# Second parts of the down projection's weights by a negating copy on ScalarE and an accumulating DMA

## The chip, the cores and the metric

The kernel runs on one core of a Trainium2 chip. The metric is the device time of one execution in microseconds (us). The profile is one execution recorded by the hardware; times inside it count from the start of its span.

## The reference, cut to what matters

Two layers of an encoder over 768 tokens of width 1024 (512 of a prompt, 256 of a sample). Each layer is a feed-forward, a mixer (a state-space recurrence and neighbourhood attention in layer 0, windowed attention in layer 1), and a second feed-forward. So the feed-forward runs four times, with a hidden width of 2816:

```python
def swiglu(x, wg, wu, wd):
    return (jax.nn.silu(x @ wg) * (x @ wu)) @ wd

for layer in range(DEPTH):
    x = x + 0.5 * swiglu(rms_norm(x, norm_ffn[layer, 0]), ...)
    ...                                   # the mixer
    x = x + 0.5 * swiglu(rms_norm(x, norm_ffn[layer, 1]), ...)
return rms_norm(x, norm_final)
```

The change touches how `wd`, the down projection's weights, come to TensorE. All inputs are float32.

## The kernel before, in words

**Two parts for each operand.** TensorE works on float32r, a float32 rounded to fewer bits. To keep the accuracy, `split` (L85) turns a float32 tile into two float32r parts: ScalarE copies it, which rounds (the first part, L88), and VectorE subtracts that copy from the source (the second part, L89). Each product is then three matmuls: first by first, and each first by the other's second.

**Weights.** A weight block of 128 x 1024 float32 (512 KB) is loaded by a DMA on SyncE's queue (SP) into a buffer `raw` (7 of them, L77). `part` (L92) splits 512 columns of it into a buffer `whl` with both parts (8 of them, L93). `weights` (L97) is a generator that yields the parts of the whole network in the order in which they are used. `take` (L187) hands out the next part and `fetch` (L180) lets the generator run ahead (`self.look`). What really bounds the running ahead is the eight `whl` buffers: a part is split when TensorE has done with the part eight places before it.

**Feed-forward.** `ffn` (L225) goes through the 22 blocks of 128 hidden features in 11 pairs, numbered 0 to 10. For a pair, the gate product has seven or eight weight parts of 12 matmuls each (L247), the up product as many. `rows` (L349) then adds the pair's share of the down projection: it takes four parts, which this text calls d0 to d3 (d0 and d1 are the two halves of the columns for the first feature block, d2 and d3 for the second), and does 72 matmuls (L362), twelve for each of six token tiles: for the left half of the columns d0 three times and d2 three times, for the right half d1 and d3. The `rows` of a pair come after the next pair's gate, so that the order on TensorE is gate of pair b, `rows` of pair b-1, up of pair b. The `rows` of pair 0 of each feed-forward are an exception in that much other work precedes them at once. Each token tile's half is added to the residual by VectorE (L365).

**GpSimd (POOL).** In the first feed-forward only, GpSimd also builds the matrices of the recurrence (`s5_matrices`, L418) in 16 rounds: some twenty small products (L579 to L595), DMAs of the results to DRAM (L600, L623, L624), while TensorE transposes its results (L605) in between its own work. In the other three feed-forwards GpSimd has nothing but a tiny operation for each norm (L199).

**Order.** The program's order on each engine is fixed by a scheduler when the kernel is built; every engine works through its own list in order, and waits by semaphores. A change of one instruction can therefore change the order of its neighbours too.

Of the kernel before, what the change touches and what calls it, by code (L numbers as in the profile page):

```python
# [11 lines left out]
F32 = mybir.dt.float32  # L12
F32R = mybir.dt.float32r
I32 = mybir.dt.int32
AF = mybir.ActivationFunctionType
ALU = mybir.AluOpType
# [3 lines left out]
P = 128  # L20
# [17 lines left out]
# neighbourhood attention: (first query, queries, first key, keys) in the order (column, row)  # L38
NA_Q = [(0, 128, 0, 256), (128, 128, 64, 256), (256, 128, 192, 256), (384, 128, 256, 256),
        (512, 128, 512, 160), (640, 128, 608, 160)]  # L40
# key blocks (first key, keys) of the windows above
# [5 lines left out]
class Trunk:  # L47
# [20 lines left out]
    def warm(self, after):  # L68
        """have the table of the square root loaded as soon as the column "after" is there"""
        w = self.cp.tile([P, 1], F32, tag="warm", name="warm", bufs=2)  # L70
        self.nc.scalar.activation(w, after, AF.Sqrt, bias=self.one, scale=0.0)
# [13 lines left out]
    def split(self, hl, lo, src):  # L85
        """hl (rounded) + lo = src, exactly"""
        nc = self.nc
        nc.scalar.copy(hl, src)  # L88
        nc.vector.tensor_sub(lo, src, hl.bitcast(F32))  # L89

# [6 lines left out]
    def weights(self):  # L97
        """the weights of the whole trunk"""
        v = self.nc.vector

        def block(n, *at):
            r = self.raw(self.a[n][at])
            for e in range(2):
                yield (n, *at, e), self.part(r[:, e * 512 : (e + 1) * 512])

        def down(q, b):
            for c in (2 * b, 2 * b + 1):
                yield from block("w_down", q, c)

        def head(n, q, b, r1):  # L110
            for e in range(2):
                yield (n, q, b, f"1{e + 1}"), self.part(r1[:, e * 512 : (e + 1) * 512])

        def quad(n, q, b, r1=None):
            """the parts and sums of two blocks of features; without the head if r1, the first, is given"""
            k = lambda z: (n, q, b, z)
            headed, r1 = r1 is not None, self.raw(self.a[n][q, 2 * b]) if r1 is None else r1
            a11, a12 = r1[:, :512], r1[:, 512:]
            if not headed:
                yield k("11"), self.part(a11)  # L120
            r2 = self.raw(self.a[n][q, 2 * b + 1])
            a21, a22 = r2[:, :512], r2[:, 512:]
            s1 = self.wp.tile([P, 512], F32, tag="st", name="st", bufs=2)
            v.tensor_add(s1, a21, a22)  # L124
            v.tensor_sub(a21, a11, a21)
            v.tensor_sub(a11, s1, a11)
            yield k("s2"), self.part(a11)
            yield k("s1"), self.part(s1)
            if b < 2:
                yield k("22"), self.part(a22)  # L130
            yield k("s3"), self.part(a21)
            if not headed:
                yield k("12"), self.part(a12)
            v.tensor_sub(a12, a12, a11)
            yield k("s4"), self.part(a12)
            if b > 1:
                yield k("22"), self.part(a22)

        def fast(q):
            both = ("w_gate", "w_up")  # L140
            first = lambda n, b: self.raw(self.a[n][q, b])
            r = {n: first(n, 0) for n in both}
            for b in range(2):
                heads = [head(n, q, b, first(n, 2) if b else r[n]) for n in both]
                for z in heads * 2:
                    yield next(z)
            for z in [quad(n, q, 0, r[n]) for n in both] * 5:
                yield next(z)
            for b in range(1, NF // 2):
                for n in both:  # L150
                    yield from quad(n, q, b, first(n, 2) if b == 1 else None)
                    if n == "w_gate":
                        yield from down(q, b - 1)
            yield from down(q, NF // 2 - 1)

        def out(n, kb, half):
            for e in range(2):
                yield from block(n, half, 2 * kb + e)

        yield from fast(0)  # L160
        for f in [0, 1, 2, 3] + [4 + e + h for h in range(4) for e in (8, 0, 4)]:
            yield from block("w_in_even", f)
        yield from out("w_out_even", 1, 0)
        for f in range(2):
            yield from block("s5_wg", f)
        for kb, half in ((1, 1), (0, 0), (0, 1)):
            yield from out("w_out_even", kb, half)
        yield from fast(1)
        yield from fast(2)
        for f in (8, 9):  # L170
            yield from block("w_in_odd", f)
        for e in range(2):
            yield from block("w_v_odd", e)
        for f in range(8):
            yield from block("w_in_odd", f)
        for kb, half in ((0, 0), (0, 1), (1, 0), (1, 1)):
            yield from out("w_out_odd", kb, half)
        yield from fast(3)
# [16 lines left out]
    def norm_half(self, t, out):  # L195
        """sum of squares of the first half of token tile t"""
# [5 lines left out]
    def norm_rows(self, t, gb, out, ss, parts=1):  # L202
        """out = rms_norm of token tile t"""
# [4 lines left out]
        for e in range(parts):  # L208
            c = slice(e * DM // parts, (e + 1) * DM // parts)
# [8 lines left out]
    def gemm(self, o, w, act, k0, n, kk=range(KM), last=KM - 1):  # L218
        """o[128 features, n tokens] = w^T act, w stationary; w and act hold four blocks of 128 features to a tile"""
# [5 lines left out]
    def ffn(self, q, norm, tail, extra=None):  # L225
        """gate and up by Winograd's form of Strassen's product over 2 blocks of features, of inputs and of tokens"""
# [4 lines left out]
        with ExitStack() as ctx:  # L231
# [18 lines left out]
            def quad(n, b, use):  # L250
                """steps of the four blocks; use(feature block, token half, value)"""
# [97 lines left out]
    def rows(self, hs, q, b, pos, tail=None):  # L349
        """steps of x += 0.5 h wd over a pair of blocks of features"""  # L350
# [22 lines left out]
    def out_pass(self, name, kb, half, act, tail=None):  # L373
        """steps of x[:, half] += act w over k-block kb (4 of 128 features); act(part, k) has all tokens"""
# [24 lines left out]
    def fgemm(self, f, hn, evac, norm=None, kk=KM):  # L399
        """steps of a feature block of act @ w, feature-major; f names the weights, evac(psum, first token, tokens)"""  # L400
# [13 lines left out]
        h = kk // 2  # L414
        return [lambda: part(0, NP, NS, range(kk)), lambda: part(1, 0, NP, range(h)), lambda: part(2, 0, NP, range(h, kk))]

# [1 line left out]
    def s5_matrices(self, pool, spare):  # L418
# [10 lines left out]
        class Room:  # L429
            """carves blocks out of tiles"""  # L430
# [26 lines left out]
        def exp(out, x):  # L457
            """exp to float32's accuracy"""
# [51 lines left out]
        # (a - 1) / lambda  # L510
# [15 lines left out]
        # powers 0..8  # L526
# [40 lines left out]
        def start(q):  # L567
            """a pair of groups: W2 (state -> outputs), W1 (inputs -> state)"""
# [28 lines left out]
        def finish(q):  # L597
            """W1 transposed, E (inputs -> outputs)"""
# [44 lines left out]
    def mixer0(self, norm, tail):  # L643
# [4 lines left out]
        with ExitStack() as ctx:  # L648
            mp = ctx.enter_context(self.tc.tile_pool(name="mix0", bufs=1))

            # inputs of S5, in (chunk position, channel) rows
# [14 lines left out]
            def qkv(h):  # L666
                """steps of a head pair's values, queries and keys, in the order (column, row)"""
# [28 lines left out]
            def na(h):  # L696
                """steps of a head pair; q is overwritten by the output, feature-major"""
# [65 lines left out]
            # chunk inputs of the states; both directions run from slot to slot, the reversed one backwards in time  # L763
# [31 lines left out]
            # outputs of S5: chunk inputs through M, states before the chunk through W2  # L795
# [54 lines left out]
            # the neighbourhood half of the output projection around the gate of S5  # L850
# [25 lines left out]
    def mixer1(self, norm, tail):  # L876
        nc, a = self.nc, self.a
        hn = norm.hn
        with ExitStack() as ctx:
# [4 lines left out]
            # a key head's two parts above each other, the first part in the rows that its queries have  # L884
# [11 lines left out]
            # (query tile, first key tile, key tiles, first column of the bias)  # L896
# [20 lines left out]
            def att(m, store):  # L917
                """steps of the heads of key heads 2m and 2m+1"""
                bias, pend, pts, qq = [] if m else [bias0], {}, [], {}

                def queries(t):
                    """the first parts twice above each other, and the second parts"""
# [146 lines left out]
def weave(main, *sides):  # L1069
    """emit the steps of main with those of the sides spread between them"""  # L1070
# [13 lines left out]
class NormOut:  # L1084
    """final rms_norm, a token tile at a time"""
# [17 lines left out]
class NormT:  # L1103
    """rms_norm, transposed to feature-major in two parts, a token tile at a time"""
# [41 lines left out]
class NormS(NormT):  # L1146
    """the same as the sums that ffn multiplies with; tokens of tiles 4, 5, 0 and of 1, 2, 3 face each other"""
# [46 lines left out]
    def rest(self):  # L1194
        """the parts that later products take, a step for each"""
# [39 lines left out]
def _na_index(t):  # L1235
    """row of the padded table for each (query, key) of query tile t"""
# [9 lines left out]
def _layout(i):  # L1246
# [13 lines left out]
    # heads of the odd layer: tile (m, r) holds head r of key heads 2m and 2m+1  # L1260
# [5 lines left out]
    # S5  # L1266
# [11 lines left out]
    # biases by constant index; the last entry of the padded table is the masked one  # L1278
# [26 lines left out]
```

## Time and profile before

| | us |
|---|---|
| time, median of 2 runs | 2751.07 (2750.31 to 2751.83) |
| span of the profiled execution | 2751.6 |
| TensorE (PE) busy | 2695.9 (98%) |
| VectorE (DVE) busy | 2008.4 (73%) |
| ScalarE (ACT) busy | 1176.3 (43%) |
| GpSimd (POOL) busy | 340.6 (12%) |
| DMA: bytes moved | 217.48 MB |

The profiled execution's span stands 0.5 us above the median of the runs, so sums made against the span hold for the median as well. Busy time of PE is modelled for the ends of its pipelined matmuls, so it says where PE had work, not how close it is to its peak. PEclk is the clock that TensorE was granted, as a share of its 2.4 GHz; 0.5 is its lower level of 1.2 GHz.

### The profile page before, as it was taken

Reading aid. Unit: us, or ns where it says so; the run is one execution under the profiler, and the core shown is the slowest. Engines: PE = TensorE matmul, PEld = TensorE weight load, DVE = VectorE, ACT = ScalarE, POOL = GpSimd, SP = SyncE. Lnnn points to the kernel's source line nnn. Section 1 sums busy time; section 2 is a strip of 40 time slices with the busy share of each in tenths; the row PEclk is TensorE's granted clock in tenths of the full one; section 3 lists DMA queues with packets and bytes.
Section 4 is the critical chain, followed back from the end, with each engine's and each line's share of the span. In section 5 each row is a group of like instructions: output and inputs, shape, how many; then the busy total and the mean of one; then the engine's idle time right before and its main releaser. Section 6 shows DMA issues by size and latency. Waiting matters only on the chain.

```text
span 2751.6 us, 38966 instructions
## 1 busy us (share of the span) xinstructions
PE 2695.9 (98%) x14636; PEld 2422.3 (88%) x14636; DVE 2008.4 (73%) x3878; ACT 1176.3 (43%) x2464; POOL 340.6 (12%) x688
## 2 busy tenths in 40 slices
PE   7999999998999999999999999999999999999998
PEld 7988988888888999999989999999876689999997
DVE  8967776772964887677789776767557678777776
ACT  6333333343565633333354333334457664333333
POOL 0156654300840000000000000000000000000000
PEclk9999999999999999999999999999999999999999
DMA  4122222316244222121203121211201123122221
GB/s 155 65 90 85 90 90 77 127 54 134 89 125 142 81 81 85 54 85 54 88 29 122 62 77 62 79 61 39 100 16 39 45 72 108 63 76 68 71 70 54
DMA packets 81245, 217.48 MB, mean 79 GB/s; under 512 B 22848, under 2 KB 29632, under 8 KB 80800
## 3 DMA queue, kind: packets, MB, share of 16 engines
q1 hardware_dynamic: 77152, 203.91, 23.4%
q0 software_dynamic: 3904, 11.08, 1.2%
q8 instruction: 115, 1.88, 0.3%
q14 instruction: 74, 0.61, 0.1%
HBM read 199.17 MB, written 17.89 MB: 79 GB/s over the span
## 4 chain that ended last, share of the span: by engine, by line
PE 92%; DVE 3%; DMA 2%; ACT 2%; POOL 1%; issue 1%; SPq 0%; DVEq 0%; ACTq 0%; POOLq 0%
PE ps L247 44%; PE ps L362 25%; PE ps L222 8%; PE ps L389 5%; PE ps L957 1%; PE ps L990 1%; PE ps L956 1%; PE ps L978 1%; PE ps L1133 1%; PE ps L1009 1%; PE ps L774 1%; PE ps L616 1%; DVE raw L210 1%; PE ps L746 1%; DVE whl L89 0%
## 5 line engine op out<-in xcount | busy, mean ns | idle before, releaser
L88 ACT CAST whl<-raw 128x512 fp32r<-128x512 f32 x796 | 480.3, 621 | 943.7 <-PE ps L362 446.6
L247 PE MATMUL ps<-bt,whl 128*128 128x384 f32 x4224 | 764.6, 336 | 8.9 <-DVE ct L273 8.9
L247 PEld LDWEIGHTS ps<-bt,whl 128*128 128x128 f32 x4224 | 737.9, 189 | 12.5 <-DVE ct L273 10.1
L362 PE MATMUL ps<-whl,hl 128*128 128x512 f32 x3168 | 732.7, 391 | 0.0
L89 DVE TENSOR_TENSOR whl<-raw,whl 128x512 fp32r<-128x512 f32 x796 | 550.6, 705 | 220.2 <-ACT whl L88 209.2
L362 PEld LDWEIGHTS ps<-whl,hl 128*128 128x128 f32 x3168 | 593.9, 188 | 123.5 <-ACT hl L88 0.9
L247 PE MATMUL ps<-b,whl 128*128 128x384 f32 x3168 | 580.3, 336 | 0.0
L247 PEld LDWEIGHTS ps<-b,whl 128*128 128x128 f32 x3168 | 555.1, 189 | 3.5 <-ACT hct L617 0.3
L365 DVE SCALAR_TENSOR_TENSOR x<-ps,x 128x512 f32<-128x512 f32 x528 | 361.5, 689 | 217.5 <-PE ps L362 215.3
L199 POOL TENSOR_SCALAR ss<-ss 128x1 f32<-128x1 f32 x42 | 11.3, 270 | 1787.2 <-ACT raw L198 1787.2
L222 PE MATMUL ps<-hn,whl 128*128 128x256 f32 (+1 forms) x1248 | 231.2, 342 | 1.4 <-ACT hn L88 1.4
L222 PEld LDWEIGHTS ps<-hn,whl 128*128 128x128 f32 x1248 | 191.8, 190 | 31.8 <-issue 3.3
L88 ACT CAST hl<-hct 128x384 fp32r<-128x384 f32 x176 | 86.9, 512 | 50.8 <-DVE hct L317 44.9
L389 PE MATMUL ps<-whl,ob 128*128 128x512 f32 x432 | 105.2, 399 | 0.0
L89 DVE TENSOR_TENSOR hl<-hct,hl 128x384 fp32r<-128x384 f32 x176 | 98.3, 577 | 7.7 <-ACT hl L88 7.4
L389 PEld LDWEIGHTS ps<-whl,ob 128*128 128x128 f32 x432 | 80.7, 190 | 19.7 <-issue 2.2
L279 ACT COPY ct<-ps 128x384 f32<-128x384 f32 x88 | 42.3, 481 | 102.4 <-PE ps L247 102.4
L314 ACT ACTIVATE hct<-ct 128x384 f32<-128x384 f32 x88 | 46.3, 526 | 91.3 <-DVE ct L285 79.9
L284 DVE TENSOR_TENSOR ct<-ps,hct 128x384 f32<-128x384 f32 x88 | 48.9, 556 | 29.3 <-PE ps L247 29.1
L124 DVE TENSOR_TENSOR st<-raw 128x512 f32<-128x512 f32 x88 | 62.6, 712 | 10.1 <-DMA raw<-in_w_gate 9.2
L958 DVE CUSTOM_DVE_ANT_0 raw<-ps,gb,sk 128x256 f32<-128x256 f32 (+1 forms) x96 | 48.6, 525 | 29.0 <-PE ps L957 25.8
L392 DVE TENSOR_TENSOR x<-ps,x 128x512 f32<-128x512 f32 x48 | 33.0, 688 | 48.6 <-PE ps L389 48.6
(235 smaller groups left out, 2632.8 us busy)
## 6 DMA issues: line engine op xcount, KB each, us to landing
raw<-in_w_gate SPq DMA_DIRECT2D x92, 512.0 KB, 3.6
raw<-in_w_up SPq DMA_DIRECT2D x92, 512.0 KB, 3.6
raw<-in_w_down SPq DMA_DIRECT2D x88, 512.0 KB, 3.7
raw<-in_w_in_even SPq DMA_DIRECT2D x16, 512.0 KB, 3.6
raw<-in_w_in_odd SPq DMA_DIRECT2D x10, 512.0 KB, 4.8
W2d<-raw POOLq DMA_DIRECT2D x16, 256.0 KB, 2.4
W1d<-hct POOLq DMA_DIRECT2D x16, 256.0 KB, 3.0
raw<-W1d SPq DMA_DIRECT2D x8, 512.0 KB, 5.5
```

What stands on the lines that cost most here:

```text
L88: nc.scalar.copy(hl, src)
L89: nc.vector.tensor_sub(lo, src, hl.bitcast(F32))
L124: v.tensor_add(s1, a21, a22)
L222: self.nc.tensor.matmul(o, w[k // 4][:, j, k % 4 * P : (k % 4 + 1) * P], act[i][k // 4][:, k % 4, k0 : k0 + n], start=k == 0 and (j, i) == ...
L247: nc.tensor.matmul(o, w[:, j, k * P : (k + 1) * P], B[z][:, i, k], start=first and k == 0 and (j, i) == (0, 0), stop=k == 3 and (j, i) == ...
L279: nc.scalar.copy(bank["r5"], bank[3])
L284: v.tensor_add(u3, bank[2], bank["p1"])
L314: nc.scalar.activation(at(f, t), o, AF.Silu)
L362: nc.tensor.matmul(o, h[i][:, pos[t] * P : (pos[t] + 1) * P], w[half][:, j], start=n == 0 and (j, i) == (0, 0), stop=n == len(hs) - 1 and ...
L365: nc.vector.scalar_tensor_tensor(xs, o, 0.5, xs, ALU.mult, ALU.add)
L389: nc.tensor.matmul(o, act(i, k)[:, t * P : (t + 1) * P], st["w"][k][:, j], start=m == 0, stop=m == 11)
L958: nc.vector.tensor_tensor_reduce(p[:, e, :n], s[:, :n], bias[0][:, par * 4 + h, c0 : c0 + n], -1.0, sk[:, 1, hh + h : hh + h + 1], ALU.add ...
```

## The change

For the down projection's weights alone, `down` no longer calls `block`. The first part is made as before. The second part's place is then filled by ScalarE with the first part negated, and a DMA issued from GpSimd adds the weights to it, read a second time from DRAM. VectorE has no part in it any more. Comments and docstrings are taken out elsewhere; lines of the changed kernel stand 8 higher than before from there on (L362 becomes L370).

```diff
         def down(q, b):
+
             for c in (2 * b, 2 * b + 1):
-                yield from block("w_down", q, c)
+                r = self.raw(self.a["w_down"][q, c])
+                for e in range(2):
+                    z = slice(e * 512, (e + 1) * 512)
+                    w = self.wp.tile([P, 2, 512], F32R, tag="whl", name="whl", bufs=8)
+                    self.nc.scalar.copy(w[:, 0], r[:, z])
+                    self.nc.scalar.activation(w[:, 1], w[:, 0].bitcast(F32), AF.Copy, scale=-1.0)
+                    self.nc.gpsimd.dma_start(w[:, 1], self.a["w_down"][q, c][:, z], accum_op=ALU.add)
+                    yield ("w_down", q, c, e), w
```

It does so 176 times: 4 feed-forwards x 11 pairs x 4 parts. The scheduler places the new instructions, and moves others. Three places matter.

**ScalarE, ahead of the first `rows` (pair 0) of the second feed-forward.** The rows of before; whl_9489, whl_9507, whl_9524 and whl_9545 are d0 to d3, and whl_9570 is a part of the next pair's gate:

```order
L88 CAST whl_9489<-raw_9487 128x512
L279 COPY ct_9504<-ps_9486 128x384
L88 CAST whl_9507<-raw_9487 128x512
L88 CAST whl_9524<-raw_9522 128x512
L88 CAST whl_9545<-raw_9522 128x512
L314 ACTIVATE hct_9048<-ct_9504 128x384
L314 ACTIVATE hct_9048<-hct_9048 128x384
L314 ACTIVATE hct_9048<-ct_9484 128x384
L88 CAST whl_9570<-raw_9562 128x512
```

And of the change, where d0 to d3 are whl_9533, whl_9552, whl_9570 and whl_9592, and the gate's part is whl_9618:

```order
L113 CAST whl_9533<-raw_9531 128x512
L287 COPY ct_9549<-ps_9530 128x384
L114 ACTIVATE whl_9533<-whl_9533 128x512
L113 CAST whl_9552<-raw_9531 128x512
L113 CAST whl_9570<-raw_9568 128x512
L114 ACTIVATE whl_9552<-whl_9552 128x512
L114 ACTIVATE whl_9570<-whl_9570 128x512
L113 CAST whl_9592<-raw_9568 128x512
L88 CAST whl_9618<-raw_9610 128x512
L322 ACTIVATE hct_9092<-ct_9549 128x384
L322 ACTIVATE hct_9092<-hct_9092 128x384
L114 ACTIVATE whl_9592<-whl_9592 128x512
```

The four negations (L114) have come in, and that of d3 stands behind the gate's cast and two activations, which wait for VectorE.

**TensorE, at the start of the same `rows`.** Before, each part is used three times running, its second part by the second of the three:

```order
L362 MATMUL ps_9582<-whl_9489,hl_9049 128x512 x3
L362 MATMUL ps_9582<-whl_9524,hl_9049 128x512 x3
L362 MATMUL ps_9590<-whl_9507,hl_9049 128x512 x3
L362 MATMUL ps_9590<-whl_9545,hl_9049 128x512 x3
L362 MATMUL ps_9598<-whl_9489,hl_9049 128x512 x3
```

The change, up to the second parts of d3 (whl_9592, the x2):

```order
L370 MATMUL ps_9630<-whl_9533,hl_9093 128x512 x3
L370 MATMUL ps_9630<-whl_9570,hl_9093 128x512
L370 MATMUL ps_9638<-whl_9552,hl_9093 128x512
L370 MATMUL ps_9646<-whl_9533,hl_9093 128x512
L370 MATMUL ps_9638<-whl_9552,hl_9093 128x512 x2
L370 MATMUL ps_9638<-whl_9592,hl_9093 128x512
L370 MATMUL ps_9646<-whl_9533,hl_9093 128x512
L370 MATMUL ps_9630<-whl_9570,hl_9093 128x512 x2
L370 MATMUL ps_9646<-whl_9533,hl_9093 128x512
L370 MATMUL ps_9646<-whl_9570,hl_9093 128x512 x3
L370 MATMUL ps_9654<-whl_9552,hl_9093 128x512 x3
L370 MATMUL ps_9638<-whl_9592,hl_9093 128x512 x2
```

The same matmuls are interleaved so that second parts are first used later: d0's still by the 2nd matmul, d1's by the 7th (before the 8th), d2's by the 11th (before the 5th), d3's by the 20th (before the 11th). The first `rows` of the other feed-forwards and the last ones (pair 10) are interleaved in a like manner; in the last `rows` of the first feed-forward d2's second part is first used by the 13th matmul and d3's by the 16th. All other `rows` keep the order of before.

**GpSimd, in the first feed-forward, ahead of the `rows` of pair 6.** Before, one round of the recurrence's matrices runs on (from its fourth large product on; raw and hct are its buffers):

```order
L586 TENSOR_TENSOR raw_985<-hct_229 128x2x128
L587 TENSOR_TENSOR hct_229<-s5k_984,raw_983 128x256
L588 TENSOR_TENSOR hct_229<-s5k_984,raw_983 128x256
L589 TENSOR_TENSOR raw_985<-hct_229 128x2x128
L590 TENSOR_TENSOR hct_229<-s5k_984,raw_983 128x256
L591 TENSOR_TENSOR hct_229<-s5k_984,raw_983 128x256
L600 DMA W2d_979<-raw_985 128x512
L592 TENSOR_TENSOR raw_985<-hct_229 128x2x128
```

With the change the four accumulating DMAs (L115) of pair 6 stand inside that round:

```order
L115 DMA whl_3554<-in_w_down 128x512
L595 TENSOR_TENSOR hct_229<-s5k_988,raw_987 128x256
L596 TENSOR_TENSOR hct_229<-s5k_988,raw_987 128x256
L597 TENSOR_TENSOR raw_989<-hct_229 128x2x128
L598 TENSOR_TENSOR hct_229<-s5k_988,raw_987 128x256
L599 TENSOR_TENSOR hct_229<-s5k_988,raw_987 128x256
L608 DMA W2d_983<-raw_989 128x512
L600 TENSOR_TENSOR raw_989<-hct_229 128x2x128
L115 DMA whl_3574<-in_w_down 128x512
L601 TENSOR_TENSOR hct_229<-s5k_988,raw_987 128x256
L602 TENSOR_TENSOR hct_229<-s5k_988,raw_987 128x256
L115 DMA whl_3593<-in_w_down 128x512
```

The DMA of d2 (whl_3593) comes just ahead of the round's last product (L603, which was L595), that of d3 right behind it. The loads on SyncE's queue stand in the same order as before.

## Rows read from the trace of the kernel before

**Rows 1.** The page's busy time and share of the span, by engine

```profile
PE 2695.9 (98%) x14636; PEld 2422.3 (88%) x14636; DVE 2008.4 (73%) x3878; ACT 1176.3 (43%) x2464; POOL 340.6 (12%) x688
```

**Rows 2.** Table by stretch: us, busy (count) of each engine, PEclk, DMA share, GB/s

```profile
100.00:200.00 100.00, 94.63 (x499) 85.48 (x498) 79.72 (x195) 31.05 (x62) 42.04 (x65) 0.95 0.23 73
1600.00:1700.00 100.00, 100.00 (x534) 94.30 (x533) 74.61 (x126) 36.19 (x69) 0.00 (x0) 1.00 0.24 78
```

**Rows 3.** PE's waits: in total, times, the longest (us)

```profile
PE ps L247 <- DVE ct L273: 8.9, 3, 4.0
PE ps L605 <- POOL raw L595: 5.7, 2, 2.9
```

**Rows 4.** Groups of instructions: count, busy us, mean ns, idle before and its releasers

```profile
L89 DVE TENSOR_TENSOR whl<-raw,whl 128x512 fp32r<-128x512 f32 x796 | 550.6, 705 | 220.2 <-ACT whl L88 209.2
L88 ACT CAST whl<-raw 128x512 fp32r<-128x512 f32 x796 | 480.3, 621 | 943.7 <-PE ps L362 446.6 <-PE ps L247 145.8 <-DVE raw L134 143.5
```

**Rows 5.** Timeline of the second feed-forward: start, us; casts of d0 and d3, their `rows`

```profile
1320.31 0.62 ACT L88 CAST whl<-raw 128x512 fp32r<-128x512 f32 x1 [1.45 <-PE ps L247]
...
1326.88 0.62 ACT L88 CAST whl<-raw 128x512 fp32r<-128x512 f32 x1
...
1334.63 16.52 PE L362 MATMUL ps<-whl,hl 128*128 128x512 f32 x72
```

**Rows 6.** DMA issues: count, KB each, median us from issue to landing

```profile
raw<-in_w_down SPq DMA_DIRECT2D x88, 512.0 KB, 3.7
W2d<-raw POOLq DMA_DIRECT2D x16, 256.0 KB, 2.4
W1d<-hct POOLq DMA_DIRECT2D x16, 256.0 KB, 3.0
...
raw<-in_w_out_even SPq DMA_DIRECT2D x8, 512.0 KB, 5.6
...
U<-Ud SPq DMA_DIRECT2D x8, 192.0 KB, 11.1
```

**Rows 7.** Chain of waits: start, us; the `rows` of pair 0, second feed-forward

```profile
974.90 16.36 PE ps L362 x72
```

**Rows 8.** Timeline of ACT, then of PE, at these `rows`

```profile
970.05 0.62 ACT L88 CAST whl<-raw 128x512 fp32r<-128x512 f32 x1
970.58 0.47 ACT L279 COPY ct<-ps 128x384 f32<-128x384 f32 x1
970.95 1.67 ACT L88 CAST whl<-raw 128x512 fp32r<-128x512 f32 x3
...
975.04 0.53 ACT L314 ACTIVATE hct<-hct 128x384 f32<-128x384 f32 x1
```

```profile
974.74 5.64 PE L362 MATMUL ps<-whl,hl 128*128 128x512 f32 x24
```

**Rows 9.** Timeline of the first feed-forward, pair 6: GpSimd's round and the `rows`

```profile
378.06 1.07 POOL L586 TENSOR_TENSOR raw<-hct 128x256 f32<-128x256 f32 x1
379.20 0.62 POOL L587 TENSOR_TENSOR hct<-s5k,raw 128x256 f32<-128x256 f32 x1
...
383.60 0.62 POOL L600 DMA_DIRECT2D W2d<-raw  x1
...
387.03 2.93 PE L362 MATMUL ps<-whl,hl 128*128 128x512 f32 x12
387.13 1.07 POOL L595 TENSOR_TENSOR raw<-hct 128x256 f32<-128x256 f32 x1
```

**Rows 10.** Timeline of the first feed-forward, pair 10: casts of d2 and d3, the `rows`

```profile
580.44 1.14 ACT L88 CAST whl<-raw 128x512 fp32r<-128x512 f32 x2
...
580.71 8.61 PE L362 MATMUL ps<-whl,hl 128*128 128x512 f32 x36
```

**Rows 11.** PE by stretch: us, busy (count), PEclk, DMA share, GB/s

```profile
139.00:143.00 4.00, 2.07 (x12) 1.00 0.84 301
143.00:147.00 4.00, 4.00 (x31) 1.00 0.00 2
218.00:222.00 4.00, 0.00 (x0) 1.00 0.09 33
222.00:227.00 5.00, 5.00 (x20) 0.66 0.63 211
...
169.00:179.00 10.00, 9.91 (x44) 0.51 0.13 41
```

## The prediction

> **What bounds the kernel now.** I read the busy times first [rows 1]: TensorE has work for 2695.9 of 2751.6 us, VectorE, which the change relieves, for 2008.4. So at most 55.7 us (2.0%) of PE's idle time is there to win by all means together. The table by stretch says where it lies [rows 2]: in the middle of a feed-forward (1600 to 1700 us) PE is busy for all of 100.00 us at full clock, while in the first feed-forward, where the matrices of the recurrence are built beside it, it is busy for 94.63 of 100 at a mean clock of 0.95. PE's waits name VectorE in that part for 8.9 us in three places, GpSimd for 5.7 [rows 3]. So work taken from VectorE shows in the time only by these 8.9 us; everywhere else the question is whether the new way of making the second parts is ready before PE wants them.
>
> **What is removed and added.** 176 subtractions of 0.705 us leave VectorE, 124 us [rows 4]. 176 negations come to ScalarE. The trace has no negation; the cast of the same shape takes 0.621 us [rows 4], so 109 us and a busy share of 47% instead of 43% [rows 1]. They are hidden by PE's matmuls as long as the parts stay early; ScalarE idles 943.7 us ahead of its casts alone, mostly waiting for PE [rows 4]. GpSimd gets 176 DMA issues; one of its DMAs of 256 KB takes 0.62 us to issue [rows 9]. The DMA traffic grows by 176 x 256 KB = 46 MB on top of 217; the engines' mean share in the middle of a feed-forward is 0.24 [rows 2], so the bandwidth is there.
>
> **The new latency.** Before, a second part is there 0.7 us after the first. Now it is a negation (0.62) and a DMA. Call L the time from the DMA's issue to its landing. No accumulating DMA stands in the trace. Below, L is 2.4 us, the quickest plain 256 KB of GpSimd's queue (another takes 3.0). The accumulating one also has to read its destination, so it handles 512 KB; the nearest row is the 512 KB load of the same weights, 3.7 us, and I take that. Above, 512 KB in a crowded stretch take 5.6, and the slowest row of all, 192 KB in small pieces, 11.1 [rows 6].
>
> The Trainium skill, "DMA: Bandwidth & Descriptors", section "Anatomy of one DMA — SWDGE (gpsimd) path", gives about 2.0 us plus bytes over 436 GB/s for a plain DMA of GpSimd, so an estimate of 2.6 us for 256 KB; the two rows of 2.4 and 3.0 agree, and no row here shows an accumulating one. By 2.6 instead of 3.7 the sum below would come to +5 us.
>
> **Pairs 1 to 9, and the last pair of the later feed-forwards: hidden.** The last part, d3, has its cast done at 1327.50, and its `rows` start at 1334.63 [rows 5]. A `rows` has 72 matmuls in 16.36 us [rows 7], 0.227 each. d3's second part is first used by the 11th, at 1336.9. After the negation, 8.8 us are left for L; d0, cast from 1320.31, has more, with the parts between. The cover is the gate product on PE. It holds up to L = 8.8.
>
> **Pair 0, four times.** Here d0's cast starts at 970.05 and the others follow to 972.62, while PE begins at 974.74 [rows 8]. By ScalarE's new order the negations end at about 971.7 (d0, behind the copy), 973.4 (d1, behind two more casts), 974.0 (d2), and d3's only behind two activations that end at 975.57 in the trace, so 976.2. By PE's new order the second parts are wanted at 974.97, 976.1, 977.0 and 979.05. That leaves 3.3, 2.7, 3.0 and 2.85 us for L, so PE waits L - 2.7 = 1.0 us. Four times, 4.0.
>
> **Pair 6 of the first feed-forward.** GpSimd's queue holds the DMAs between its products. In the trace L595 starts at 387.13 [rows 9]; with three DMAs of 0.62 ahead of it and 1.07 for itself, d3's is issued at 390.06 and lands at 393.8. PE wants it with the 11th matmul, at 387.03 + 2.3 = 389.3. It waits 4.4 us. In the other rounds the DMAs stand earlier before their `rows`; pair 5's last one is the closest, and I count nothing for it.
>
> **Pair 10 of the first feed-forward.** ScalarE's list has the casts of d2 and d3 behind the up product's last steps: 580.44 to 581.58, with PE at `rows` from 580.71 [rows 10]. Both casts, then d2's negation: issue at 582.2, landing at 585.9; wanted by the 13th matmul at 583.4. PE waits 2.5 us.
>
> **What a wait costs beyond itself.** After an idle gap of 1.93 us in 139 to 143 the granted clock stayed 1.00; after 4 us idle it fell to a mean of 0.66 for 5 us (1.7 us lost), and in another place to 0.51 for 10 us (4.9 lost) [rows 11]. 0.5 is the 1.2 GHz level. I count one such fall, after pair 6, at the middle, 3.3 us. The waits at pair 0 come in two pieces, and that of pair 10 lies between.
>
> **What VectorE gives back.** PE's 4.0 us wait for L273 ends at 222 us, and the four subtractions of pair 3 are in VectorE's list around it; without them L273 comes 4 x 0.705 = 2.8 us earlier. Bounds: nothing, and all 8.9 us of such waits [rows 3].
>
> **Sum.** 4.0 + 4.4 + 2.5 + 3.3 - 2.8 = +11.4 us on the span's 2751.6, which stands 0.5 above the median: 2751.1 + 11.4 = about 2762 us. That is 0.4%. A change of under 2% (55 us) is about what a measurement of this kernel can't tell from none.
>
> **Rivals.**
> 1. *The parts come early anyway.* With L = 2.4 the pair 0 waits vanish, pair 6 costs 3.1, pair 10 costs 1.2, no clock falls, and VectorE's 8.9 us come back: 4.3 - 8.9 = -4.6, 2746 us. For it: GpSimd's plain rows. Against: the destination is read as well. A gain over 2% has no place to come from [rows 1].
> 2. *The accumulating DMA is slow.* One mechanism, L. At 5.6 the same sum is 4 x 2.9 + 6.3 + 4.4 = 22.3, with a full clock fall at each of the six places 29.4 more: 2803. From L = 6.2 on with the falls, it is slower by over 2%. Past 8.8 all other `rows` wait too: at 11.1, 38 x 2.3 = 87 on top of 33.6 + 11.8 + 9.9, and 44 falls of at least 1.7: about 2970. For it: no row shows what adding in flight costs. Against: the transfers are full rows of 2 KB, unlike the small pieces of the 11.1.
> 3. *GpSimd is kept from issuing by VectorE.* A GpSimd product takes 0.62 us in one place and 1.07 in another of the same round [rows 9]. If each issue grows by that 0.45, pair 6 waits 4 x 0.45 longer, the five others 0.45: +4, 2766. The Trainium skill warns of it in "SBUF — State Buffer", section "SBUF: two separate sides": while VectorE runs an operation in a 2-port mode, GpSimd can't write its descriptors. By that rule the change would suffer most where VectorE is busiest; the trace has a DMA issue of 0.62 us in a round whose products were stretched, so I give it little.
>
> **How the numbers follow.** My forecast 0.66, rival 1 0.13, rival 2 0.17, rival 3 0.04. The first three reach from 2746 (all of rival 1) to 2803 (rival 2's milder end); I take 2746 to 2808, which leaves out the worse part of rival 2 and a few percent below. Over 2% slower is rival 2 from L = 6.2: 0.16. Over 2% faster: 0.01. The rest, 0.83, is within 2%.
>
> **What would show it.** The median landing of the accumulating DMAs is L: under 4 with me, over 6 with rival 2. PE's waits should name that DMA or its landing at the first `rows` of each feed-forward, 1 us each, and in pairs 6 and 10 of the first; the middle of the later feed-forwards should still have PE busy for 100 of 100 us. The wait for L273 should shrink, and VectorE's busy time fall to about 1884. If PE waits in every pair, L is past 8.8 and the forecast is wrong. If GpSimd's issues take much more than 0.62 us, its rounds in the first feed-forward become late and PE's wait for L595 grows, which my sum leaves out.

## The result and the profile after

The change takes 2781.76 us (median of two runs, 2778.65 to 2784.87) against 2751.07: 1.0109 times the time before, 95% interval 1.0088 to 1.0129, or +30.7 us. The profiled execution has a span of 2783.1, 31.5 above that of before. The forecast was 2762 in a range of 2746 to 2808, so the time lies inside the range and within 2%; but its sum of +11.4 is little over a third of what came.

Busy time by engine, and DMA queue q0 (GpSimd's: packets, MB, share of the 16 DMA engines' time), from the page of the change:

```profile
PE 2711.4 (97%) x14636; PEld 2429.1 (87%) x14636; DVE 1897.0 (68%) x3702; ACT 1276.3 (46%) x2640; POOL 480.6 (17%) x864
q0 software_dynamic: 29248, 57.23, 11.2%
```

Against [rows 1], TensorE is busy for 15.5 us more with the same 14636 matmuls, and idle for 71.7 us instead of 55.7. Half of the loss shows as waiting and half as slower work; of the slower work 11 us are time at the lower clock (worked out from the granted clock over TensorE's busy time in both traces). This is a split by where the time shows, not by cause: at pair 0, below, slower matmuls stand in the place of further waits. VectorE has lost 111 us of work, as intended.

TensorE's waits in the change (in total, times, the longest), which answer to [rows 3]:

```profile
PE ps L370 <- DMA whl<-in_w_down: 26.2, 15, 4.0
...
PE ps L613 <- POOL raw L603: 3.9, 2, 2.6
...
PE ps L255 <- DVE ct L281: 1.8, 2, 1.3
```

There is a new wait of 26.2 us, in 15 pieces, for the accumulating DMAs. The wait for VectorE has shrunk from 8.9 to 1.8, that for GpSimd from 5.7 to 3.9.

The new groups of instructions, and the DMA issues (count, KB each, median us from issue to landing), which answer to [rows 4, 6]:

```profile
L115 POOL DMA_DIRECT2D whl<-in_w_down x176 | 154.4, 914 | 1507.0 <-DVE hl L89 881.5
...
L114 ACT ACTIVATE whl<-whl 128x512 fp32r<-128x512 f32 x176 | 110.5, 631 | 3.9
```

```profile
raw<-in_w_down SPq DMA_DIRECT2D x88, 512.0 KB, 4.3
whl<-in_w_down POOLq DMA_DIRECT2D x176, 256.0 KB, 5.9
...
W2d<-raw POOLq DMA_DIRECT2D x16, 256.0 KB, 2.4
W1d<-hct POOLq DMA_DIRECT2D x16, 256.0 KB, 5.4
```

The negation takes 0.631 us (0.62 was taken from the cast). L, the time from issue to landing, is 5.9 us in the median, not 3.7; it ranges from 3.6 to 9.1. The other transfers land later too: the weight loads went from 3.7 to 4.3, GpSimd's W1d from 3.0 to 5.4 (of which a part, 3.9, comes without any of the new transfers, see below).

The table by stretch that answers to [rows 2] (us, busy of PE, PEld, DVE, ACT, POOL, then PEclk, DMA share, GB/s):

```profile
100.00:200.00 100.00, 97.43 (x534) 89.95 (x534) 78.02 (x189) 38.46 (x74) 44.28 (x73) 0.98 0.35 94
1600.00:1700.00 100.00, 100.00 (x523) 93.07 (x523) 68.33 (x113) 38.28 (x72) 6.90 (x8) 1.00 0.32 85
```

In the middle of a feed-forward TensorE still has no gap. In the first feed-forward it has fewer than before (97.43 busy against 94.63).

**Where the 31.5 us of span are.** For each of the 44 `rows` I took the end of its last matmul in both traces; the table gives how much the distance to before grew from one `rows` to the next (us, worked out from these ends). The entry of pair 0 also holds all that lies between two feed-forwards, which in the kernels below that leave pair 0 alone differs from before by -1.4 to +6.4 in single executions. The `rows` of pair 0 by themselves are longer by 7.4, 6.2, 6.7 and 8.1, which is 28.3 in sum.

| place | the change | the prediction's term |
|---|---|---|
| pair 0 of the four feed-forwards | +7.4, +4.6, +6.7, +9.9 = +28.5 | +4.0 |
| first feed-forward, pairs 1 to 3 | -10.5 | -2.8 |
| pair 5 | +8.1 | 0 |
| pair 6 | +3.7 | +4.4, and +3.3 for the clock |
| pairs 7 to 9 | -5.8 | 0 |
| pair 10 | +7.4 | +2.5 |
| pair 4, and all other pairs of the later three | +0.1 | 0 |

### The profile page after: what moved, and what is told of

Read it like the earlier page. It is cut to its first block, busy times and chain, and to the rows that moved or that the text cites. A ratio compares the mean times of both kernels' runs of the same rounds, so it can differ in the third digit from the quotient of the medians.

```text
span 2783.1 us, 39413 instructions
## 1 busy us (share of the span) xinstructions
PE 2711.4 (97%) x14636; PEld 2429.1 (87%) x14636; DVE 1897.0 (68%) x3702; ACT 1276.3 (46%) x2640; POOL 480.6 (17%) x864
## 3 DMA queue, kind: packets, MB, share of 16 engines
q1 hardware_dynamic: 77152, 203.91, 22.8%
q0 software_dynamic: 29248, 57.23, 11.2%
## 4 chain that ended last, share of the span: by engine, by line
PE 87%; DMA 4%; DVE 3%; issue 2%; ACT 2%; POOL 2%; SPq 0%; DVEq 0%; POOLq 0%; ACTq 0%
PE ps L255 40%; PE ps L370 25%; PE ps L230 8%; PE ps L397 5%; DMA whl<-in_w_down 2%; PE ps L965 1%; PE ps L998 1%; PE ps L964 1%; PE ps L986 1%; PE ps L1141 1%; DVE whl L89 1%; PE ps L782 1%; PE ps L1017 1%; DVE raw L218 1%; DMA W1d<-hct 1%
## 5 line engine op out<-in xcount | busy, mean ns | idle before, releaser
L370 PE MATMUL ps<-whl,hl 128*128 128x512 f32 x3168 | 750.4, 396 | 26.4 <-DMA whl<-in_w_down 26.2
L370 PEld LDWEIGHTS ps<-whl,hl 128*128 128x128 f32 x3168 | 601.5, 191 | 159.8 <-DMA whl<-in_w_down 34.9
L89 DVE TENSOR_TENSOR whl<-raw,whl 128x512 fp32r<-128x512 f32 x620 | 426.3, 702 | 174.5 <-ACT whl L88 162.4
L115 POOL DMA_DIRECT2D whl<-in_w_down x176 | 154.4, 914 | 1507.0 <-DVE hl L89 881.5
L292 DVE TENSOR_TENSOR ct<-ps,hct 128x384 f32<-128x384 f32 x88 | 48.9, 556 | 127.0 <-PE ps L255 126.8
L114 ACT ACTIVATE whl<-whl 128x512 fp32r<-128x512 f32 x176 | 110.5, 631 | 3.9
L281 DVE TENSOR_TENSOR ct<-ps,hct 128x384 f32<-128x384 f32 x88 | 49.0, 557 | 47.3 <-PE ps L255 47.1
```

The source lines that it names most:

```text
L114: self.nc.scalar.activation(w[:, 1], w[:, 0].bitcast(F32), AF.Copy, scale=-1.0)
L115: self.nc.gpsimd.dma_start(w[:, 1], self.a["w_down"][q, c][:, z], accum_op=ALU.add)
L281: v.tensor_add(bank["u2"], bank[2], bank["p1"])
L292: v.tensor_add(u3, bank[2], bank["p1"])
L370: nc.tensor.matmul(o, h[i][:, pos[t] * P : (pos[t] + 1) * P], w[half][:, j], start=n == 0 and (j, i) == (0, 0), stop=n == len(hs) - 1 and ...
```

## Pair 0 in the trace of the change

Pair 0 of the second feed-forward, the place of [rows 8]: timeline of GpSimd (start, us, and idle time before with its releaser), then of TensorE.

```profile
980.61 0.96 POOL L115 DMA_DIRECT2D whl<-in_w_down  x1 [51.31 <-DVE st L132]
982.17 1.76 POOL L115 DMA_DIRECT2D whl<-in_w_down  x2 [0.60 <-DVE ct L292]
985.06 0.86 POOL L115 DMA_DIRECT2D whl<-in_w_down  x1 [1.13 <-ACT whl L114]
```

```profile
983.46 0.40 PE L370 MATMUL ps<-whl,hl 128*128 128x512 f32 x1
987.37 2.07 PE L370 MATMUL ps<-whl,hl 128*128 128x512 f32 x5 [3.51 <-DMA whl<-in_w_down]
989.64 16.50 PE L370 MATMUL ps<-whl,hl 128*128 128x512 f32 x66 [0.20 <-DMA whl<-in_w_down]
```

The issues stand 2.9, 1.3 and 0.7 us ahead of the `rows` and 1.6 behind their start. The prediction had 3.0, 1.3, 0.7 and 1.5, so its reading of ScalarE's order was right to 0.2 us. What was wrong is L: 6.7, 7.4, 8.2 and 8.7 us for the four. Already the second matmul waits 3.5 us for d0. Here is why (TensorE by stretch: us, busy, PEclk, DMA share, GB/s):

```profile
980.00:981.50 1.50, 1.50 (x10) 1.00 0.75 188
981.50:983.00 1.50, 1.50 (x11) 1.00 1.03 209
983.00:986.00 3.00, 0.86 (x5) 1.00 0.85 226
986.00:989.00 3.00, 1.63 (x5) 0.82 1.07 284
989.00:991.00 2.00, 1.79 (x5) 0.50 1.13 208
991.00:993.00 2.00, 2.00 (x9) 0.92 0.88 295
```

The 16 DMA engines are full, a share of 0.75 to 1.13 for 13 us (a packet counts with its whole time in the stretch in which it starts, so a share can pass 1): two 512 KB weight loads, and then a third, are in flight beside the four transfers. Before, the same place had this:

```profile
972.50:974.00 1.50, 1.50 (x10) 1.00 0.92 281
974.00:977.00 3.00, 3.00 (x16) 1.00 0.76 231
977.00:980.00 3.00, 3.00 (x15) 1.00 0.24 96
```

The loads alone all but filled the engines for 4.5 us, and nobody waited. After TensorE's wait the granted clock is 0.50, its 1.2 GHz level, in the stretch from 989 on, and 1.00 again from 993. These `rows` take 22.68 us instead of 16.52: 3.7 us of waits and 2.5 of slower matmuls. In the other three feed-forwards they take 23.88, 23.20 and 24.64.

The slower matmuls cost less here than it seems. d3's second part landed 10.3 us behind the start of the `rows` (1.6 + 8.7), and the 53 matmuls from its first use, the 20th, to the end take 12.0 us at full clock (0.227 each, as in [rows 7]). So by this estimate these `rows` couldn't have ended before 22.3 us at any clock: TensorE would have waited longer for d1 to d3. The landing of d3 alone explains 5.8 of the 6.2 us lost here, and by the same working 5.6 of 6.7 in the third feed-forward and 6.2 of 8.1 in the fourth.

## The experiments

Theory: the loss sits at single places, where an accumulating DMA lands late (pair 0 everywhere; pairs 5, 6 and 10 of the first feed-forward), and VectorE's relief in the first feed-forward gives part of it back. Main rivals: ScalarE's 176 negations and the new orders cost the time; and, for L, adding in flight against mere crowding. All edits are in `down`. Where a line `if not (...)` is added, the parts that the brackets name are made in the new way, and all others by `self.split(w[:, 0], w[:, 1], r[:, z])` as before (the three lines under the `if` that do this are left out here). Ratios are to the kernel before, with 95% intervals. The places are given as in the table above.

**Without the DMA.**

```diff
-                    self.nc.gpsimd.dma_start(w[:, 1], self.a["w_down"][q, c][:, z], accum_op=ALU.add)
```

> The 176 negations stay and the accumulating DMAs are left out, so the second parts are only the negated first parts and the subtraction is not done: the time of the change without the transfer. Theory (the landing of the DMA is what is late): a second part is then there 0.63 us after its first, as before, and VectorE is relieved: -16 us, about 2735. Rival (ScalarE's 110 us of negations, and the order that they force on it and on TensorE): still near +31, 2780.

2737.78 against 2748.78 us: 0.9959 (0.9946 to 0.9973). The negations on ScalarE cost nothing, so the rival is out, and it is the transfer that turns a gain of 11 us into a loss of 31. (The scheduler orders this kernel anew, so the exact orders of the change aren't tested by it; the kernels below with 148 and with 28 parts in the new way, both faster than before, speak against a cost of them too.) The waits of this kernel:

```profile
PE ps L612 <- POOL raw L602: 2.8, 2, 2.1
...
PE ps L254 <- DVE ct L280: 1.8, 2, 1.3
```

In its trace pairs 1 to 3 gain 9.7 us and pairs 7 to 9 gain 8.5, and the late places lose nothing; its span is 2732.6. So VectorE's relief is worth far more than the 2.8 us of the sum: 7.1 us of waits for it, 2.9 of the waits for GpSimd's last product (L595 before, L602 here; 5.7 in [rows 3]), and the slower matmuls behind those waits (TensorE is busy for 6.6 us less). That is one execution against one, 19.0 us apart; the medians of the runs are 11 us apart.

**A DMA that doesn't add.**

```diff
-                    self.nc.gpsimd.dma_start(w[:, 1], self.a["w_down"][q, c][:, z], accum_op=ALU.add)
+                    self.nc.gpsimd.dma_start(w[:, 1], self.a["w_down"][q, c][:, z])
```

> The DMA of each second part stays but does not accumulate, so the weights themselves stand in the second part and the subtraction is not done: same issues, same bytes from DRAM, no adding. Theory 1 (adding makes the transfer slow): the time from issue to landing falls from 5.9 us to about 2.6, the waits at pair 0 fall to a third, and what is left is GpSimd's queue at pairs 5, 6 and 10 of the first feed-forward (+15) against VectorE's relief (-16): 2752 us. Theory 2 (the transfers are slow since four of them and the loads of the weights meet): issue to landing stays above 5 us and the time at about 2775 to 2782.

2761.66 us: 1.0045 (1.0032 to 1.0057), +12.9. From its page, queue q0 and the landing:

```profile
q0 software_dynamic: 29248, 57.23, 7.1%
whl<-in_w_down POOLq DMA_DIRECT2D x176, 256.0 KB, 3.8
```

Both theories hold a part. Adding costs some 18 of the 30.7 us, and L falls to 3.8, though not to 2.6: the quickest of the 176 takes 2.69, against 3.62 of the adding ones. The Trainium skill's "DMA: Bandwidth & Descriptors", section "Anatomy of one DMA — SWDGE (gpsimd) path", from which the prediction worked out an estimate of 2.6 us, agrees with the quickest alone. What remains is crowding by other transfers: pair 0 of the later three still loses 13.0 us, with L at 4.8 to 7.5 there, and pair 5 loses 6.6.

The queue's share also gives a price. In the change q0 has 11.2% of 2783.1 us, before 1.2% of 2751.6: 279 us of all 16 engines for 176 transfers, 1.58 us each. Plain ones take (7.1% of 2761.4 - 33.0) / 176 = 0.93, where 33.0 is the 1.2% of before. One pair asks for 6.3 us of every DMA engine, and the two loads of pair 0 take 1.6 each (the load queue's 22.8% for 203.91 MB).

**One of four parts.**

```diff
+                    if not (c == 2 * b and e == 0):
```

> Only d0 of each pair is made in the new way, 44 of the 176 parts, so no accumulating DMA has another one beside it, while the weight loads go on as they do. Theory 1 (the accumulating DMAs slow each other): issue to landing falls to 3.7 to 4.0 us in the median. Theory 2 (the weight loads slow them): it stays above 5. Pair 0 by theory 1: issue 2.9 us ahead, wanted 0.2 us behind the start of the rows, so TensorE waits 0.7 us each time, +3 us, against a fraction of VectorE's relief: 2746 to 2754 us; by theory 2 it waits 2.5 and more each time, with falls of the clock: 2757 to 2765.

2758.89 against 2752.24 us: 1.0029 (1.0018 to 1.0040). L by its page (its q0 has 3.8%, which by the same working is 1.63 us a transfer, so the price of 1.58 isn't one of their crowding each other):

```profile
whl<-in_w_down POOLq DMA_DIRECT2D x44, 256.0 KB, 4.1
```

By L theory 1 is right in the median (4.1 without neighbours of its own kind), by time theory 2: at pair 0 of the later three L is 6.4 to 6.5 with no second accumulating DMA anywhere near. TensorE's `rows` at that of the second feed-forward, and the stretches around its wait, read

```profile
972.62 18.01 PE L374 MATMUL ps<-whl,hl 128*128 128x512 f32 x71 [3.33 <-DMA whl<-in_w_down]
```

```profile
969.00:972.00 3.00, 0.30 (x2) 1.00 1.01 325
972.00:975.00 3.00, 2.38 (x7) 0.71 0.18 72
```

a full share of 1.01 by one small transfer and the weight loads. So in the middle of a feed-forward the transfers slow each other; at pair 0 the loads are enough. (No run moved the loads away; that they are the cause rests on the share, and on 6.4 here against 4.1 elsewhere.) Since no other part is late here, this kernel also shows what the clock costs: waits of 3.2 to 3.3 us lengthen these `rows` by 5.1 to 6.3 us.

**The first feed-forward alone.**

```diff
+                    if not (q == 0):
```

> Only the first feed-forward makes its second parts in the new way, the other three in the old one. Theory (late landings at single places): the trace of the change has the first feed-forward at +10 us in sum (late parts at pairs 0, 5, 6 and 10: +27; VectorE's relief at pairs 1 to 3, 7 and 8: -16), so 2761 us, and no wait for a weight part at the first rows of the three others. Rival (ScalarE's extra negations and the new order on it cost a little in each pair): a quarter of the +31 by number, +8 us, with the loss spread over all eleven pairs instead of the four places.

2765.18 against 2748.78 us: 1.0060 (1.0047 to 1.0073), +16.4 where +10 was expected; its span +11.8. The loss stands at the four places, +6.1, +8.8, +8.4 and +3.9, and the relief is -13.1. The middle pairs of the three others stand as before. The clock decides much of how a late place comes out: pair 6 costs 8.4 here, with a mean clock of 0.63 in the 5 us after its wait of 3.2, and 3.7 in the change, with 1.00 after a wait of 2.5; pair 10, after like waits, costs 3.9 here and 7.4 there.

**All but pair 0.**

```diff
+                    if not (b > 0):
```

> The change everywhere but in pair 0 of the four feed-forwards. Theory: pair 0 carries 7.4 + 4.6 + 6.7 + 9.9 = 28.5 of the change's +31.5 us of span, so +3 remain (pairs 5, 6 and 10 of the first feed-forward against VectorE's relief): 2754 us. Rival (pair 0 only shows first what ScalarE's load would cost elsewhere): the waits appear at pair 1 instead, and +15 or more remain.

2755.55 against 2752.24 us: 1.0013 (1.0002 to 1.0023), +3.3 where +3 was expected. Pair 0 carries some 27 of the 31 us, and its waits don't move on to pair 1.

**Pair 5 alone.**

```diff
+                    if not (q == 0 and b == 5):
```

> Only the four parts of pair 5 of the first feed-forward are made in the new way. In the trace of the change, GpSimd waits there for the landing of one of its own transfers to DRAM, and the issues of d2 and d3 stand in its list behind the products that follow. Theory (its place in GpSimd's list makes pair 5 late, whatever the other pairs do): its rows are about 7 us longer in the trace, and the time is +7 us, 2758. Rival (it is late since the other pairs' transfers and issues have already set GpSimd back): nothing, 2751.

2758.52 against 2750.70 us: 1.0022 (1.0012 to 1.0033), +7.8, and in the trace the place costs 7.6. It is late by itself. GpSimd's timeline there:

```profile
321.86 0.94 POOL L119 DMA_DIRECT2D whl<-in_w_down  x1 [5.34 <-ACT whl L118]
...
323.76 0.56 POOL L635 DMA_DIRECT2D W1d<-hct  x1 [0.38 <-ACT hct L618]
...
325.81 0.99 POOL L119 DMA_DIRECT2D whl<-in_w_down  x1
330.41 0.78 POOL L591 TENSOR_TENSOR hct<-s5k 128x32 f32<-128x32 f32 x1 [3.61 <-DMA W1d<-hct]
...
333.97 0.89 POOL L119 DMA_DIRECT2D whl<-in_w_down  x1
...
339.36 0.89 POOL L119 DMA_DIRECT2D whl<-in_w_down  x1
```

And its `rows` on TensorE:

```profile
335.10 1.08 PE L374 MATMUL ps<-whl,hl 128*128 128x512 f32 x4
337.79 1.65 PE L374 MATMUL ps<-whl,hl 128*128 128x512 f32 x6 [1.60 <-DMA whl<-in_w_down]
343.26 7.78 PE L374 MATMUL ps<-whl,hl 128*128 128x512 f32 x26 [3.81 <-DMA whl<-in_w_down]
```

GpSimd can't begin the next round before its own W1d has left the buffer. In the kernel before that wait is

```profile
327.31 0.24 POOL L579 TENSOR_TENSOR hct<-s5k 128x32 f32<-128x32 f32 x1 [0.16 <-DMA W1d<-hct]
```

0.16 us; here it is 3.61. The new transfers are not what brings it: in the kernel without any of them the same wait is

```profile
319.41 0.78 POOL L586 TENSOR_TENSOR hct<-s5k 128x32 f32<-128x32 f32 x1 [3.06 <-DMA W1d<-hct]
```

What has moved is a weight load. SyncE's two loads of gate weights at this place, first in the kernel before, then in that without the DMA (each line spans from the first load's start to the second's end):

```profile
321.03 5.20 SPq L79 DMA_DIRECT2D raw<-in_w_gate  x2
```

```profile
310.57 3.30 SPq L79 DMA_DIRECT2D raw<-in_w_gate  x2
```

The second of the two waits for its buffer. Before, that wait ends with VectorE (L619) after 4.6 us, and the load is issued 1.1 us behind W1d. In the new way VectorE no longer reads the down projection's weights; the wait ends with ScalarE's cast after 2.6 us, and the load is issued 0.8 us ahead of W1d. In the five kernels here with the load 1.1 us behind, W1d lands in 2.4 us; in the six with it 0.8 us ahead, in 5.0 to 6.9, whether the new transfers are there or not. (With one part of four it is 0.5 us behind, and W1d takes 4.6.) So the round comes about 3 us late, and d2's and d3's DMAs stand in it: d3 is issued 4.3 us after its `rows` began and takes 3.9. The late issue is due to GpSimd's own wait and to its place in the list, and hardly to L; with plain transfers the place still loses 6.6 us.

**Added twice.** In pairs 1 to 10 of the last three feed-forwards:

```diff
+                    if not (q > 0 and b > 0):
...
                     self.nc.gpsimd.dma_start(w[:, 1], self.a["w_down"][q, c][:, z], accum_op=ALU.add)
+                    self.nc.gpsimd.dma_start(w[:, 1], self.a["w_down"][q, c][:, z], accum_op=ALU.add)
```

> In pairs 1 to 10 of the last three feed-forwards the accumulating DMA is issued twice, one behind the other, so the second parts hold the weights once too often; all other parts are made in the old way. It asks how much time the gate product covers. By the trace of the change d3 is issued 6.2 us ahead of the rows and wanted 2.3 us behind their start, 8.5 us for a landing. Theory: two landings in a row take about 12, so TensorE waits about 3.5 us or more in each of some 30 pairs, +105 us at least, with falls of the clock up to +250: 2855 to 3000 us. Rival (the cover is larger than that, since the scheduler or ScalarE can run further ahead): below +50.

One execution, 2953.51 us, a span of 2951.7, +200. TensorE's wait, and its timeline in a middle pair:

```profile
PE ps L375 <- DMA whl<-in_w_down: 133.5, 42, 6.7
```

```profile
1115.46 1.08 PE L375 MATMUL ps<-whl,hl 128*128 128x512 f32 x4
1120.84 2.92 PE L375 MATMUL ps<-whl,hl 128*128 128x512 f32 x6 [4.29 <-DMA whl<-in_w_down]
1124.13 14.41 PE L375 MATMUL ps<-whl,hl 128*128 128x512 f32 x62 [0.38 <-DMA whl<-in_w_down]
```

The cover is finite: each of the 30 `rows` now loses 4.0 to 8.9 us, 133.5 in all by waiting and most of the rest at the lower clock. This is not a clean measure of the cover's length, since the second issue waits on GpSimd for the first landing and holds up the next part's.

**Not at the late places.**

```diff
+                    if not (b > 0 and not (q == 0 and b in (5, 6, 10))):
```

> The change everywhere but in pair 0 of each feed-forward and pairs 5, 6 and 10 of the first one: 148 of the 176 parts are still made in the new way. Theory: the late places are gone and VectorE's relief in the first feed-forward stays, -16 us: 2735 us, and the middle pairs of the later feed-forwards stand where they stood. Rival (ScalarE's extra work and order): 148 of 176 negations remain, so +26 us, 2777.

2740.11 us: 0.9967 (0.9955 to 0.9980), faster than before by 8.7 us with 148 parts made in the new way, near the bound set by the kernel without any DMA. In the trace pairs 1 to 3 give -11.0, pairs 7 to 9 -6.7, and all middle pairs of the later feed-forwards 0.0, with L at 5.8 in the median. 16 us had been expected. The relief is that large in the profiled execution (span -13.7), less in the median of the runs.

**Only where it pays.**

```diff
+                    if not (q == 0 and b in (1, 2, 3, 4, 7, 8, 9)):
```

> The new way only in pairs 1 to 4 and 7 to 9 of the first feed-forward, 28 of 176 parts; all others as before. Theory (the only gain is VectorE's relief there, and the hidden parts elsewhere are worth nothing): as the kernel without the late places, -8 to -14 us, about 2739. Rival (VectorE's relief in the other feed-forwards carries part of that gain): -5 or less.

2740.31 against 2752.24 us: 0.9962 (0.9949 to 0.9975). 28 parts give what 148 give, so the relief outside the first feed-forward is worth nothing. (Its profiled execution has a span of 2748.1; 9.5 us of that stand between the feed-forwards, where nothing was edited.)

**Three pairs.**

```diff
+                    if not (q == 0 and b in (2, 3, 7)):
```

> The new way only in pairs 2, 3 and 7 of the first feed-forward, 12 of 176 parts: those ahead of whose rows the trace of before has TensorE's longest waits for VectorE and for GpSimd's L595. Theory (the relief works only where TensorE waits for VectorE's list, or for products that VectorE stretches): -8 us or more, near the 28 parts of pairs 1 to 4 and 7 to 9, 2741. Rival (VectorE's backlog is carried from pair to pair, so that the relief has to be there before): -4 or less.

2746.17 against 2750.70 us: 0.9981 (0.9972 to 0.9989), -4.5, which is near the rival's -4 and short of the theory's -8. By the medians the pairs next to TensorE's waits carry about half of the gain (0.9981 beside 0.9962, with intervals that touch). The profiled executions give them more: pairs 1 to 3 and 7 to 9 gain 10.5 us here and 12.8 with 28 parts. So their share isn't settled, and how VectorE's backlog passes from pair to pair was not followed further. With 12 parts this is the smallest edit that is still faster than the kernel before.

## Why the prediction was right and wrong

**Right: what bounds the kernel, and where the new way shows.** TensorE kept its bound. The middle pairs stayed hidden to 0.0 us although L came out at 5.9, as the slack of 8.8 us said; the nearest landing came 0.4 us ahead of its use. The places named (pair 0, pairs 6 and 10) are late. The negation's cost, and at pair 0 its place on ScalarE and the times of the issues, were right to 0.2 us; the kernel without the DMA shows that ScalarE's part is indeed free. An issue record of 0.91 us in the mean looks longer than the 0.62 assumed, but in a series the next instruction mostly starts 0.54 to 0.67 us after the last (at pair 0, 1.76 us hold two records that overlap).

**Wrong: L, the first term.** "The engines' mean share in the middle of a feed-forward is 0.24, so the bandwidth is there" is the step that failed. That share is a mean over 100 us; at pair 0, where the transfers are wanted at once, [rows 8] have the four casts within 2.6 us, and the loads that refill the buffers come at that moment. The trace of before could have told it: a share of 0.92 and 0.76 in the stretches around 974. Adding in flight then costs 1.58 us of all engines where a plain transfer costs 0.93. The formula itself held: with each part's own L in place of 3.7 its waits are 3.4 us for d0 (6.7 - 3.3), 4.7, 5.2 and 5.8 for d3 (8.7 - 2.85); the longest counts, 5.8, and these `rows` lost 6.2. Pair 0 was undersized by 24.5 us; the whole sum fell 20.1 short, since the other errors partly cancel.

**Wrong: where the clock falls.** One fall was counted, 3.3 us after pair 6. There it didn't come: after waits of 2.45 and 0.52 us the granted clock stayed at 1.00 for the next 15 us. It came where none was counted: to 0.50 after the 3.5 us at pair 0, and to a mean of 0.50 and of 0.66 over the 5 us after the waits of pairs 5 and 10. At pair 0 it added little to what the late landings cost anyway, as worked out above; at pair 10 the waits are only 2.4 of the 7.4 us.

**Right by luck: the waits of pairs 6 and 10.** At pair 6 d3 was put 3.0 us behind the start of its `rows` (390.06 against 387.03), to wait 4.4 us. In the change it is issued 0.7 us behind, the longer wait is one for d2, and both come to 3.0. At pair 10 the waits come to 2.4 where 2.5 was said, but at the 19th and 23rd matmul and not at the 13th, and with L at 4.1 and 5.8.

**Wrong: pair 5, counted as nothing.** The issues were placed by GpSimd's times in the trace before. Those times depend on the loads, which the change moves: a weight load comes 1.9 us earlier because VectorE no longer holds its buffer, and the wait for W1d went from 0.16 to some 3 us. The prediction named late rounds of GpSimd as a risk, but looked for them at TensorE's wait for L595, which shrank; they came back in the parts that queue behind the round.

**Wrong: VectorE's relief.** Taken as 2.8 us, one wait; it was 16 us in the trace of the change, and 9 to 12 us by the medians of the kernels that keep the relief without the late places. The waits for L273 shrank from 8.9 to 1.8 us, GpSimd's products came earlier too, and the clock falls behind those waits (part of them in [rows 2]'s mean of 0.95) went with them. In the traces it hid 13.5 of the 33.6 us by which the other terms fell short; that the time still lies inside the range is partly owed to this.

**The rivals.** Rival 2 (a slow accumulating DMA) had the mechanism: at L = 5.6 it said 2803, on the assumption that all six places pay a full fall of the clock. With a measured median of 5.9 the time was 2782: the relief was larger than it allowed, and the falls cost less. Rival 3 didn't show: in a series an issue takes about the 0.62 us assumed, and what kept GpSimd from issuing at pair 5 was a transfer, not VectorE.

## What to carry to other kernels

Read the DMA engines' share in the few microseconds in which a transfer is wanted, not over the stage: a transfer that is free in the steady state can be late where a stage starts and its buffers are refilled. When an engine no longer reads a buffer, the next load into it starts sooner: ask which transfer that load then meets, who waits for its landing, and what is queued behind that wait. When several parts are late at once, a lower clock and a wait can hide in each other; work out when the last part lands before giving time to either. Work taken off an engine pays only where something waits for it, so apply such an edit at those places alone; here 28 of 176 parts gave all the gain.

## What was not expected of the hardware

- An accumulating DMA of 256 KB takes 3.6 us at the quickest, 5.9 in the median and 9.1 at worst from issue to landing; the same transfer without adding 2.7, 3.8 and 7.5. It holds the 16 DMA engines for 1.58 us instead of 0.93.
- With one part late at pair 0 (one of four parts), a wait of 3.2 to 3.3 us on TensorE made a step of 16.5 us 5.1 to 6.3 us longer; the granted clock was 0.50 in a stretch of 2 us soon after the wait.
- GpSimd's 256 KB to DRAM landed in 2.4 us with a 512 KB load issued 1.1 us behind it, and in 5.0 us with that load 0.8 us ahead of it.
